# Hybrid SSD and attention block: operand of the SSD half of the output projection made during the last input unit, results of the last four column blocks in tiles of the weight pool

## The chip, the cores and the metric

One core of one Trainium2 chip runs the whole program. The metric is the device time of one execution in microseconds (us); lower is better. Engines are named as in the profile: PE (matrix products), PEld (its weight loads), ACT, DVE, POOL (element-wise engines), SP (issues most DMAs).

## The reference, cut to what matters

One block of a network on 512 tokens of width 2048, all in float32. The output projection (`mixed @ w_out`) is the part that the change touches.

```python
u = rmsnorm(h, attn_norm_w)
z, xbc, dt_raw, q, kc, vc, ks, vs, kw, vw, gate_raw = split(u @ w_in)
y_ssd = ssd_mixer(z, xbc, dt_raw, ...)      # rmsnorm(y * silu(z), norm_w), width 1024
y_att = nsa_mixer(q, kc, vc, ks, vs, ...)   # three-branch attention, 16 heads of 64, width 1024
mixed = concatenate([y_ssd, y_att], -1)     # width 2048
h = h + mixed @ w_out
v = rmsnorm(h, ffn_norm_w)
h = h + (silu(v @ w_gate) * (v @ w_up)) @ w_down
return rmsnorm(h, final_norm_w)
```

## The kernel before

**Products.** Each float32 operand is split into a high part (hi) and a remainder (lo). One 128-deep slice k of a product is three matmuls of 128x128 by 128x512: hi by hi (L234), hi by lo (L235), lo by hi (L236). The moving operand stands in the tile `U`, 16 slices with a hi and a lo each (`u` in the profile's rows).

**Stages.** First come 41 input units, one for each block of 128 columns of w_in, with 16 slices each. Then come 16 output units, one for each block c of 128 columns of w_out. Output unit c covers only its first NS[c] slices (11 or 12 of 16, 8 for the last): slices 0 to 7 are the SSD half, from 8 on the attention half. The remaining slices of w_out follow as steps 0 to 15 (`run_step`; L1177 to L1179 are their matmuls), which run from another set of tiles. Gate, up and down products come last.

**Weights.** Blocks of four slices (256 KB) are loaded on SP's queue (L200) into `wraw` tiles of the pool `wp`, tag "raw", four buffers. ACT makes `whi` (L125), DVE makes `wlo` (L128). Splits run three blocks ahead of PE, loads three blocks further. The steps load their weights into `Z` (L1112 on SP), ACT and DVE split them into `R`.

**Other work.** SSD, token compression and attention are tasks in one list. PE's program runs one slice, then `sch.tick()` lets each task go on if its count of slices is over (`yield n` waits n slices). So the attention of the last group of heads runs between the slices of the first output units. PE takes its instructions in the order in which they are written; on the other engines a scheduler places them. An engine takes its queue strictly in order.

**The SSD half of the operand.** `pre_out` runs ahead of output unit 0. For each k of 0 to 7 it loads a 256 KB slice `gy_d[k]` from memory on SP's queue (L967) into a tile `gy` of the same four "raw" buffers as the weights, POOL multiplies it by a row (L134), ACT scales it by a column and makes the hi (L125, `u<-gy,colc`), DVE makes the lo (L970). `ma_in` does the like for the attention half, from `at_d` (L977).

**Results of output units.** `ev_os(c)` copies the sum from PSUM to a tile `h1` (L989, ACT), adds the residual x by an accumulating DMA on POOL's queue (L990), and four slices later writes `h1_d[c]` by another DMA on POOL's queue (L992); the profile shows `h1_d` and `h_d` both as `h_d`, `h1` as `h`. For c up to 14 the tile is `yz` in the attention pool `att`, one buffer; for c = 15, when that pool is closed, it is a piece of the tile `A` of the next pool. `pre_last`, ahead of output unit 15, closes `att` and opens the pool with `A`, `Z`, `R`, and `R` takes memory in which the `yz` buffer lay. Step c then loads `h1_d[c]` back (L1222), adds its own sum (L137) and writes `h_d` on POOL's queue (L1228).

Of the kernel before, what the change touches and what calls it, by code (L numbers as in the profile page):

```python
# [8 lines left out]
F32 = mybir.dt.float32  # L9
# [6 lines left out]
KD = D // 128  # L16
# [14 lines left out]
PACE_OUT = [1,2,1,2]  # L31
# [36 lines left out]
U_VS = [25, 29, 33, 37]  # L68
# [47 lines left out]
def body(ctx, tc, xT, w_in, w_out, w_gate, w_up, w_down, w1k, w1v, cols, rows, kst, out):  # L116
    nc = tc.nc
    act, dve, pool, pe = nc.scalar, nc.vector, nc.gpsimd, nc.tensor
    sch = Sched()

    def f(ap):
        return ap.bitcast(F32)

    def a_hi(dst, src, scale=1.0):
        act.activation(dst, src, AF.Copy, scale=scale)  # L125

    def lo(eng, dst, src, hi):
        eng.tensor_tensor(dst, src, f(hi), ALU.subtract)  # L128
# [4 lines left out]
    def mul(eng, o, a, b):  # L133
        eng.tensor_tensor(o, a, b, ALU.mult)  # L134
# [33 lines left out]
    pools = {}  # L168

    def open_pool(name, stack=None, **kw):  # L170
        es = ExitStack()
        pools[name] = (es, es.enter_context(tc.tile_pool(name=name, bufs=1, reuse_waits="tile", **kw)))
        return pools[name][1]
# [19 lines left out]
    raw, hi_t, lo_t = {}, {}, {}  # L193
# [78 lines left out]
    def col(c, n=1):  # L272
        return colc[:, c:c + n]
# [25 lines left out]
    U = up.tile([128, 2, KD, 512], F32R, name="u")  # L299
    wp = open_pool("wp", side="right")  # L300
# [282 lines left out]
    P2 = {}  # L583
# [333 lines left out]
    def win(u):  # L917
        return w_in[u]

    ev = {U_DTG: ev_dtg}  # L920
# [28 lines left out]
    order = [U_DTG]  # L949
# [3 lines left out]
    for g in range(4):  # L953
        z = {0: [], 1: [4, 5], 2: [6], 3: [7]}[g]
        order += [U_Z[t] for t in z] + [U_VS[g], U_KS[g]] + U_Q[g]
    units = [Unit(win(u), KD, u_rhs, ev[u], pre=pre_att if u == U_VS[0] else None) for u in order]


    def pre_out():
        P2["pace"] = PACE_OUT  # L960
        sch.run_until(*[("gy", t) for t in range(8)])
        P2["ms"] = [(U[:, 0, k], U[:, 1, k]) for k in range(8)]
        P2["ma"] = [(U[:, 0, 8 + k], U[:, 1, 8 + k]) for k in range(8)]
        for k in range(8):
            h_, l_ = P2["ms"][k]
            t = wp.tile([128, 512], F32, tag="raw", name="gy", bufs=4)
            nc.sync.dma_start(t, gy_d[k])  # L967
            mul(pool, t, t, P2["row2"])
            a_hi(h_, t, scale=col(C_SN + k))
            dve.scalar_tensor_tensor(l_, t, col(C_SN + k), f(h_), op0=ALU.mult, op1=ALU.subtract)  # L970
        sch.add(ma_in(P2["at"] + 1))

    def ma_in(n):

        for k in range(n):
            h_, l_ = P2["ma"][k]
            nc.sync.dma_start(f(l_), at_d[k])  # L977
            yield 1 if k < 4 else 8
            a_hi(h_, f(l_))
            lo(dve, l_, f(l_), h_)  # L980
            sch.flags.add(("ma", k))

    def ev_os(c):
        def ev(p):
            if "att" in pools:
                t = pools["att"][1].tile([128, 512], F32, tag="yz", name="h1", bufs=1)
            else:
                t = P2["TT"][:, 2 * (c % 2):2 * (c % 2) + 2].rearrange("p a t -> p (a t)")
            act.activation(t, p, AF.Copy)  # L989
            nc.gpsimd.dma_start(t, xT[c], accum_op=ALU.add)  # L990
            yield 4
            nc.gpsimd.dma_start(h1_d[c], t)  # L992
        return ev

    def os_rhs(k):
        if k >= 8:
            assert ("ma", k - 8) in sch.flags
        return (P2["ms"] + P2["ma"])[k]

    def pre_last():  # L1000
# [10 lines left out]
    for c in range(KD):  # L1011
        units.append(Unit(w_out[c][:, 0:NS[c], :], NS[c], os_rhs, ev_os(c),
                          pre={0: pre_out, KD - 1: pre_last}.get(c)))
# [752 lines left out]
    for k in range(KD):  # L1766
        if k % 4 == 0:
            issue_split(k // 4)
        t = xt[:, k, :]
# [5 lines left out]
    for k in range(KD):  # L1775
        t = xt[:, k, :]
# [125 lines left out]
```

## Time and profile before

| | |
|---|---|
| runs, us | 2260.8, 2263.28, 2266.31 |
| median, us | 2263.28 |
| profiled execution, us | 2260.72 |
| its span, us | 2259.0 |
| mean granted PE clock | 0.984 |
| last input unit, us from the span's start | about 600 to 612 |
| output units | 614 to 829 |
| steps 0 to 15 | from 836 |

All positions below are microseconds from the start of the span. The profile has one row for one or several equal instructions: start, duration, engine, line, operation, tiles, shape, and in brackets how long the engine had been idle before it and on what that idle time ended. A granted clock of 1.00 is full speed of PE, 0.50 is half.

### The profile page before, as it was taken

What the parts mean: (1) busy time and instruction counts of PE and PEld (TensorE: products, weight loads), DVE (VectorE), ACT (ScalarE), POOL (GpSimd) and SP (SyncE); (2) the same over time, 40 slices, a digit from 0 to 9 for tenths busy, and PEclk for the clock granted to TensorE, in tenths of its full rate; (3) what the DMA queues carried; (4) which work ended last, traced back from release to release, by engine and by line L of the source; (5) the groups of instructions that cost most, each with busy time, mean ns of one, the idle gap of its engine ahead of it and who ended that gap; (6) DMA issues with size and microseconds to landing.
All of it is one profiled execution on the core that took longest, in us unless ns stands there. A gap on an engine that the chain in (4) does not pass through costs nothing. (4 is left out here: it accounts for less than half of the span.)

```text
span 2259.0 us, 34978 instructions
## 1 busy us (share of the span) xinstructions
PE 2173.3 (96%) x12892; PEld 1908.9 (85%) x12892; DVE 1799.4 (80%) x2821; ACT 1196.9 (53%) x1991; POOL 435.3 (19%) x439
## 2 busy tenths in 40 slices
PE   7999999999989989999999999999999899999996
PEld 5888888888778877888888888888888889999996
DVE  7699766778786638988888888888887878888896
ACT  4564456666666636655555555555555433433453
POOL 2011224323331116100000000000000121221232
PEclk8999999999979999999999999999999999999999
DMA  5222343222234357787878888888887869696975
GB/s 177 89 71 75 121 150 101 78 81 73 86 87 116 105 149 228 216 235 220 240 217 251 230 237 234 219 243 218 250 230 228 322 217 312 179 292 170 306 185 139
DMA packets 170492, 416.66 MB, mean 184 GB/s; under 512 B 16800, under 2 KB 23984, under 8 KB 170320
## 3 DMA queue, kind: packets, MB, share of 16 engines
q1 hardware_dynamic: 98912, 246.73, 33.4%
q0 software_dynamic: 28112, 80.65, 18.5%
q10 hardware_dynamic: 43296, 87.04, 10.6%
q8 instruction: 101, 1.65, 0.3%
q14 instruction: 71, 0.58, 0.1%
HBM read 353.54 MB, written 57.15 MB: 182 GB/s over the span
## 5 line engine op out<-in xcount | busy, mean ns | idle before, releaser
L125 ACT ACTIVATE R<-Z 128x1024 fp32r<-128x1024 f32 (+4 forms) x458 | 415.9, 922 | 449.0 <-DVE Z L137 314.6
L128 DVE TENSOR_TENSOR R<-Z,R 128x1024 fp32r<-128x1024 f32 (+4 forms) x367 | 385.5, 1059 | 42.7 <-ACT R L125 35.0
L234 PE MATMUL ps_g<-u,whi 128*128 128x512 f32 x778 | 317.5, 408 | 3.9 <-ACT u L125 3.9
L235 PE MATMUL ps_g<-u,whi 128*128 128x512 f32 x778 | 308.3, 396 | 2.7 <-DVE u L970 2.6
L236 PE MATMUL ps_g<-u,wlo 128*128 128x512 f32 x778 | 308.9, 397 | 0.0
L1173 PE MATMUL ps_s<-u,R 128*128 128x512 f32 (+1 forms) x1160 | 253.1, 348 | 9.2 <-ACT A L1383 9.0
L128 DVE TENSOR_TENSOR wlo<-wraw,whi 128x512 fp32r<-128x512 f32 x211 | 158.4, 752 | 81.5 <-ACT whi L125 79.5
L1173 PEld LDWEIGHTS ps_s<-u,R 128*128 128x128 f32 x1160 | 187.6, 188 | 41.5 <-ACT A L1383 15.1
L125 ACT ACTIVATE whi<-wraw 128x512 fp32r<-128x512 f32 x211 | 132.0, 625 | 145.5 <-PE ps_g L235 97.2
L236 PEld LDWEIGHTS ps_g<-u,wlo 128*128 128x128 f32 x778 | 147.2, 189 | 30.4
L234 PEld LDWEIGHTS ps_g<-u,whi 128*128 128x128 f32 x778 | 147.8, 190 | 29.2 <-ACT u L125 4.4
L235 PEld LDWEIGHTS ps_g<-u,whi 128*128 128x128 f32 x778 | 147.6, 190 | 29.4 <-DVE u L970 5.7
L1173 PE MATMUL ps_t<-u,R 128*128 128x512 f32 (+1 forms) x600 | 131.4, 347 | 0.0
L1173 PE MATMUL ps_g<-u,R 128*128 128x512 f32 x584 | 131.3, 349 | 0.0
L1173 PE MATMUL ps_s<-T,R 128*128 128x512 f32 (+1 forms) x560 | 125.7, 349 | 1.6 <-DVE R L128 1.6
L1173 PE MATMUL ps_g<-T,R 128*128 128x512 f32 (+1 forms) x584 | 125.7, 346 | 0.0
L1173 PE MATMUL ps_s<-V,R 128*128 128x512 f32 (+1 forms) x568 | 123.6, 347 | 1.4 <-ACT V L125 1.1
L125 ACT ACTIVATE R<-A 128x1024 fp32r<-128x1024 f32 (+3 forms) x76 | 71.0, 934 | 86.6 <-DVE A L137 61.5
L128 DVE TENSOR_TENSOR E<-Z,R 128x1024 fp32r<-128x1024 f32 (+1 forms) x91 | 111.5, 1225 | 1.4 <-ACT R L125 1.0
L137 DVE TENSOR_TENSOR A<-ps_g,A 128x512 f32<-128x512 f32 (+1 forms) x110 | 71.1, 653 | 50.8 <-PE ps_g L1173 39.1
L1173 PEld LDWEIGHTS ps_t<-u,R 128*128 128x128 f32 x600 | 98.0, 188 | 14.1
L137 DVE TENSOR_TENSOR Z<-Z 128x1024 f32<-128x1024 f32 (+5 forms) x96 | 104.2, 1085 | 6.9 <-POOL E L137 3.9
(490 smaller groups left out, 5622.9 us busy)
## 6 DMA issues: line engine op xcount, KB each, us to landing
Z<-in_w_up SPq DMA_DIRECT2D x94, 512.0 KB, 5.3
Z<-in_w_gate SPq DMA_DIRECT2D x94, 512.0 KB, 6.5
wraw<-in_w_in SPq DMA_DIRECT2D x164, 256.0 KB, 2.6
g_d<-A ACTq DMA_DIRECT2D x22, 1792.0 KB, 15.1
Z<-in_w_up POOLq DMA_DIRECT2D x37, 512.0 KB, 8.5
Z<-in_w_gate POOLq DMA_DIRECT2D x37, 512.0 KB, 7.5
Z<-in_w_down SPq DMA_DIRECT2D x59, 320.0 KB, 5.5
Z<-in_w_down SPq DMA_DIRECT2D x41, 384.0 KB, 4.1
```

The source lines that it names most:

```text
L125: act.activation(dst, src, AF.Copy, scale=scale)
L128: eng.tensor_tensor(dst, src, f(hi), ALU.subtract)
L137: eng.tensor_tensor(o, a, b, ALU.add)
L234: pe.matmul(p, hi_t[i][:, j, :], ah, start=(k == 0), stop=False)
L235: pe.matmul(p, hi_t[i][:, j, :], al, start=False, stop=False)
L236: pe.matmul(p, lo_t[i][:, j, :], ah, start=False, stop=(k == u.nk - 1))
L1173: pe.matmul(o, w, x, start=start, stop=(k == n - 1 and o is q), skip_group_check=not fresh[0])
```

## The change

The eight SSD slices are no longer made in `pre_out`. When the last input unit starts, a task `ms_in` is added, which makes slice k two ticks after slice k-1. `os_rhs` now asserts that slice k has been made when PE's program asks for it. `ev_os` puts the results of c = 12 to 15 into a "raw" buffer of `wp`; those up to 11 stay in `yz`. Lines from 957 on move by up to 8: L967 becomes L969, L970 L972, L977 L985, L989 L997, L990 L998, L992 L1000; lines of the steps move by 7 (L1112 to L1119, L1177 to L1184, L1222 to L1229, L1228 to L1235).

```diff
-    units = [Unit(win(u), KD, u_rhs, ev[u], pre=pre_att if u == U_VS[0] else None) for u in order]
-    def pre_out():
-        P2["pace"] = PACE_OUT
-        sch.run_until(*[("gy", t) for t in range(8)])
+    units = [Unit(win(u), KD, u_rhs, ev[u], pre=pre_att if u == U_VS[0] else (lambda: pre_ms()) if u == order[-1] else None) for u in order]
+    def pre_ms():
         P2["ms"] = [(U[:, 0, k], U[:, 1, k]) for k in range(8)]
-        P2["ma"] = [(U[:, 0, 8 + k], U[:, 1, 8 + k]) for k in range(8)]
+        sch.add(ms_in())
+
+    def ms_in():
+        assert "r2" in sch.flags
         for k in range(8):
+            yield 2
             h_, l_ = P2["ms"][k]
             t = wp.tile([128, 512], F32, tag="raw", name="gy", bufs=4)
             nc.sync.dma_start(t, gy_d[k])
             mul(pool, t, t, P2["row2"])
             a_hi(h_, t, scale=col(C_SN + k))
             dve.scalar_tensor_tensor(l_, t, col(C_SN + k), f(h_), op0=ALU.mult, op1=ALU.subtract)
+            sch.flags.add(("ms", k))
+
+    def pre_out():
+        P2["pace"] = PACE_OUT
+        sch.run_until(*[("gy", t) for t in range(8)])
+        P2["ma"] = [(U[:, 0, 8 + k], U[:, 1, 8 + k]) for k in range(8)]
         sch.add(ma_in(P2["at"] + 1))
...
-            if "att" in pools:
+            if c >= 12:
+                t = wp.tile([128, 512], F32, tag="raw", name="h1", bufs=4)
+            else:
                 t = pools["att"][1].tile([128, 512], F32, tag="yz", name="h1", bufs=1)
-            else:
-                t = P2["TT"][:, 2 * (c % 2):2 * (c % 2) + 2].rearrange("p a t -> p (a t)")
             act.activation(t, p, AF.Copy)
...
-        if k >= 8:
-            assert ("ma", k - 8) in sch.flags
+        assert (("ma", k - 8) if k >= 8 else ("ms", k)) in sch.flags
```

The order of instructions moves in two places. The first is the border between the last input unit and output unit 0. On POOL, before (`uq`, `ro` and `sw` are attention's query work, `at` an attention result):

```order
L128 TENSOR_TENSOR uq<-qt,uq 64x512 x2
L134 TENSOR_TENSOR gy<-gy,row_5629 128x512
L715 DMA sw_3156<-qt 8x512
L716 DMA sw_3156<-qt 8x512
L715 DMA sw_3156<-qt 8x512
L716 DMA sw_3156<-qt 8x512
L134 TENSOR_TENSOR gy<-gy,row_5629 128x512
L896 DMA at_d<-at 128x512
L134 TENSOR_TENSOR ro_6328<-sw_3158,kc 128x512
L134 TENSOR_TENSOR gy<-gy,row_5629 128x512
L128 TENSOR_TENSOR uq<-qt,uq 64x512
```

and after:

```order
L128 TENSOR_TENSOR uq<-qt,uq 64x512 x2
L134 TENSOR_TENSOR gy<-gy,row_5629 128x512 x4
L715 DMA sw_3156<-qt 8x512
L716 DMA sw_3156<-qt 8x512
L715 DMA sw_3156<-qt 8x512
L716 DMA sw_3156<-qt 8x512
L134 TENSOR_TENSOR gy<-gy,row_5629 128x512 x2
L896 DMA at_d<-at 128x512
L134 TENSOR_TENSOR ro_6333<-sw_3158,kc 128x512
L128 TENSOR_TENSOR uq<-qt,uq 64x512
```

Four of the eight multiplications now stand ahead of the four `sw` DMAs (one before), six ahead of the next `uq` (three before), and the last two a few rows behind it.

On SP the loads of the slices move up between the loads of weights (`wraw`) and of attention results (`u<-at_d`); `-` rows stand before only, `+` rows after only:

```order
 L200 DMA wraw<-in_w_out 128x384
-L200 DMA wraw<-in_w_out 128x512 x2
-L977 DMA u<-at_d 128x512 x2
+L969 DMA gy<-gy_d 128x512 x2
+L985 DMA u<-at_d 128x512 x2
+L200 DMA wraw<-in_w_out 128x512
+L985 DMA u<-at_d 128x512
+L969 DMA gy<-gy_d 128x512 x2
+L200 DMA wraw<-in_w_out 128x512
+L969 DMA gy<-gy_d 128x512 x2
 L200 DMA wraw<-in_w_out 128x384
```

Two blocks of weights of output unit 1 that were loaded ahead of all the slices are now loaded behind some, the first behind slices 0 and 1, the second behind slices 0 to 3; all go through the same four buffers.

On PE the first slices of output unit 0 move up into the attention work of the last input unit (`ps_s` are its scores, `ps_v` its products with the values):

```order
 L236 MATMUL ps_g<-u,wlo 128x512
+L234 MATMUL ps_g<-u,whi 128x512
+L235 MATMUL ps_g<-u,whi 128x512
+L236 MATMUL ps_g<-u,wlo 128x512
+L234 MATMUL ps_g<-u,whi 128x512
 L834 MATMUL ps_s<-kh,rq 128x384
 L835 MATMUL ps_s<-kl,rq 128x384
 L879 MATMUL ps_v<-pth,v 128x512
+L235 MATMUL ps_g<-u,whi 128x512
+L236 MATMUL ps_g<-u,wlo 128x512
 L879 MATMUL ps_v<-ptl,v 128x512
```

Slice 0 and slice 1 are now written ahead of this head's scores and products; from slice 2 on, PE's order is the same in both programs: slice 2 stands behind a set of 16 small matmuls of the query work, which needs the `uq` that POOL makes.

The second place is the passage from output unit 15 to step 0. On ACT, before (`h1_8458` is the result of c = 13, `h1_8507` of 14, `A_8516` here takes that of 15):

```order
L989 ACTIVATE h1_8458<-ps_g_8378 128x512
L125 ACTIVATE whi_8479<-wraw_8415 128x512
L989 ACTIVATE h1_8507<-ps_g_8461 128x512
L1222 DMA A_8516<-h1_d_66 128x512 x3
L125 ACTIVATE R_8518<-Z_8517 128x640
L989 ACTIVATE A_8516<-ps_g_8537 128x512
L125 ACTIVATE R_8518<-Z_8517 128x640
```

and after:

```order
L997 ACTIVATE h1_8458<-ps_g_8378 128x512
L1229 DMA A_8516<-h1_d_66 128x512 x3
L125 ACTIVATE whi_8479<-wraw_8415 128x512
L125 ACTIVATE R_8518<-Z_8517 128x640 x2
L125 ACTIVATE R_8518<-Z_8517 128x512 x2
L997 ACTIVATE h1_8507<-ps_g_8461 128x512
L125 ACTIVATE E_8523<-Z_8517 128x512
L997 ACTIVATE h1_8566<-ps_g_8537 128x512
```

Before, the first `R<-Z` waits for the write of c = 14 (`yz` lay where `R` lies), and the copy of c = 14 waits for the write of c = 13 (one buffer). After, the first `R<-Z` waits for the write of c = 11, four of them stand ahead of the copy of c = 14, and that copy waits for no write. POOL's queue now has the two accumulating DMAs of c = 14 and 15, then their two writes, then the first write of `h_d` (L1235).

## The prediction, made before the changed kernel had run

> **What bounds the kernel now.** I read the page's first section, then its slices, then a table of windows around the two places that the change touches, then the timeline of each engine there.
>
> ```profile
> span 2259.0 us, 34978 instructions
> PE 2173.3 (96%) x12892; PEld 1908.9 (85%) x12892; DVE 1799.4 (80%) x2821; ACT 1196.9 (53%) x1991; POOL 435.3 (19%) x439
> ...
> PE   7999999999989989999999999999999899999996
> ...
> PEclk8999999999979999999999999999999999999999
> ```
>
> PE is busy 96% of the span, so a time can only fall where PE idles or runs at a lower clock. A slice is 56.5 us. Two of the few slices in which PE is below 9 are the twelfth (621 to 678, where the clock is also 0.7) and the fifteenth (791 to 847). These hold the start of output unit 0 and the passage to the steps. The windows (PE, PEld, DVE, ACT, POOL busy, granted clock, DMA share, GB/s):
>
> ```profile
> 590.00:612.00 22.00, 22.00 (x117) 18.72 (x115) 16.57 (x46) 17.12 (x40) 8.15 (x8) 1.00 0.33 104
> 612.00:652.00 40.00, 31.97 (x110) 24.63 (x110) 35.65 (x67) 19.84 (x46) 23.45 (x19) 0.62 0.31 87
> ...
> 829.00:842.00 13.00, 5.90 (x16) 4.25 (x15) 2.73 (x4) 3.53 (x7) 1.43 (x2) 0.61 0.73 206
> ```
>
> The last input unit (590 to 612) has PE full at full clock, with DVE idle 5.4 us and POOL 13.9. Then PE runs 110 matmuls in 40 us at a clock of 0.62, against 117 in 22 us before that: at the rate of the first window (0.19 us a matmul) that is about 21 us of work, so some 19 us are lost. In this window DVE is 89% busy and POOL more than half. The passage at 829 to 842 has 5.9 us of PE in 13.
>
> **Part 1: the SSD slices earlier.** The rows of these slices, from one answer on the tile `gy`, and where PE stood:
>
> ```profile
> L134 POOL TENSOR_TENSOR gy<-gy,row x8: 1270/1364/1752, 612.1 to 641.7; 128x512 f32<-128x512 f32 x8
> L125 ACT ACTIVATE u<-gy,colc x8: 705/710/722, 613.4 to 644.2; 128x512 fp32r<-128x512 f32 x8
> L970 DVE SCALAR_TENSOR_TENSOR u<-gy,colc,u x8: 650/744/1560, 615.4 to 645.2; 128x512 fp32r<-128x512 f32 x8
> ...
>   POOL gy L134: 10.7, 4
> ...
> DMA to landing us min/median/max: 2.7/2.7/2.8
> ```
>
> ```profile
> 614.16 0.50 PE L234 MATMUL ps_g<-u,whi 128*128 128x512 f32 x1 [1.54 <-ACT u L125]
> ...
> 629.29 0.34 PE L776 MATMUL ps_m<-kch,uq 128*128 128x32 f32 x1
> ...
> 632.46 0.37 PE L777 MATMUL ps_m<-kcl,uq 128*128 128x32 f32 x1
> ...
> 640.78 0.79 PE L234 MATMUL ps_g<-u,whi 128*128 128x512 f32 x1 [2.35 <-ACT u L125]
> ...
> 644.48 0.80 PE L235 MATMUL ps_g<-u,whi 128*128 128x512 f32 x1 [0.78 <-DVE u L970]
> ...
> 651.74 0.40 PE L236 MATMUL ps_g<-u,wlo 128*128 128x512 f32 x1
> ```
>
> Today the eight slices are made between 612.1 and 645.9, each by 2.7 us of load, 1.27 to 1.75 on POOL, 0.71 on ACT, 0.74 on DVE; POOL waits 10.7 us for loads. PE waits for them at 614, 640 and 644, and unit 0 ends at 652.1.
>
> After, four POOL multiplications stand ahead of the four `sw` DMAs, which ran at 614.33 below. They move into the last input unit, 4 x 1.27 = 5.1 us in POOL's 13.9 idle, with 4 x 0.71 on ACT (4.9 idle) and 4 x 0.74 = 3.0 on DVE (5.4 idle): cost nothing, covered by a full PE whose operands are split three blocks ahead. If that cover fails, each microsecond that DVE lacks is one of PE. The eight loads pass two weight blocks on SP; those are wanted by unit 1, after 640, some 20 us after they land: nothing.
>
> The next bound is `uq`, which releases the 16 small matmuls at 629 to 632:
>
> ```profile
> 614.33 0.53 POOL L715 DMA_DIRECT2D sw<-qt  x1 [0.98 <-DVE qt L134]
> ...
> 624.21 1.62 POOL L128 TENSOR_TENSOR uq<-qt,uq 64x512 fp32r<-64x512 f32 x1 [2.41 <-ACT uq L125]
> ...
> 627.32 1.61 POOL L128 TENSOR_TENSOR uq<-qt,uq 64x512 fp32r<-64x512 f32 x1
> ```
>
> The `uq` at 624.21 waits for ACT, and that for attention work on DVE, which loses one 0.74 us operation ahead of it; the multiplications do not hold it. I let the pair move up by 1 us, so `uq` is there at 627.9 instead of 628.9 and the small matmuls end at 631.8 instead of 632.8. From slice 2 on PE's order is as before; slices 2 to 10 are 27 matmuls, 0.23 us apart at full clock (828.65 and 828.88 below), 6.2 us, with 1.7 for the scores and transposes between them, and 1 us because the clock is still low at the start: 640.7. That is 11.4 earlier than 652.1. DVE's attention work is then the next thing late: the last two slices' lo and the attention's own operations still share it, and two lo operations (2 x 0.7 = 1.4) come off the gain. **Term: 10 us.** From below: only three of the eight lo operations leave the stretch in which DVE is full, 3 x 0.74, about 2 us; nothing excludes that. From above: the 19 us of the window. A loss is possible only as rival E. I take the value that follows from the chain of rows, between the two.
>
> **Part 2: results of c = 12 to 15 in the weight pool.** Copies and DMAs are the same in number; only what they wait for changes, so their own cost is nothing. The chain at the passage:
>
> ```profile
> 828.65 0.39 PE L235 MATMUL ps_g<-u,whi 128*128 128x512 f32 x1
> 828.88 0.39 PE L236 MATMUL ps_g<-u,wlo 128*128 128x512 f32 x1
> 836.37 0.80 PE L1177 MATMUL ps_g<-u,R 128*128 128x512 f32 x1 [7.10 <-ACT R L125]
> ...
> 841.66 0.43 PE L1177 MATMUL ps_g<-u,R 128*128 128x512 f32 x1
> ```
>
> ```profile
> 818.25 0.63 ACT L125 ACTIVATE whi<-wraw 128x512 fp32r<-128x512 f32 x1 [1.60 <-issue]
> 825.58 0.60 ACT L989 ACTIVATE h<-ps_g 128x512 f32<-128x512 f32 x1 [6.69 <-DMA h_d<-h]
> 825.60 1.30 ACTq L1222 DMA_DIRECT2D A<-h_d  x3
> 835.58 0.74 ACT L125 ACTIVATE R<-Z 128x640 fp32r<-128x640 f32 x1 [9.40 <-DMA h_d<-h]
> ```
>
> ```profile
> 814.25 1.75 SPq L1112 DMA_DIRECT2D Z<-in_w_out  x4
> ...
> 826.47 0.87 POOL L990 DMA_DIRECT2D h<-in_xT  x1 [3.07 <-ACT h L989]
> 832.39 0.56 POOL L992 DMA_DIRECT2D h_d<-h  x1 [5.05 <-DMA h<-in_xT]
> 837.10 0.87 POOL L990 DMA_DIRECT2D A<-in_xT  x1 [4.15 <-ACT A L989]
> 842.39 0.56 POOL L992 DMA_DIRECT2D h_d<-A  x1 [4.42 <-DMA A<-in_xT]
> 843.58 0.54 POOL L1228 DMA_DIRECT2D h_d<-A  x1 [0.62 <-DVE A L137]
> ```
>
> ACT waits 6.69 us for the write of c = 13 into the one buffer, copies c = 14, and waits 9.40 us for its write before it may fill `R`; PE idles 7.10 us. The Z loads were issued at 814.25 to 816.0, and such loads land about 4 us later, so the data are there at 820. After, the first `R` waits only for the write of c = 11, long past, and stands behind the `whi` of 818.25 (0.63 us): four `R` and their lo parts are made by about 823, six ahead of PE's need at 829.3. The idle 7.10 goes. With it goes the slow clock: the 12 matmuls from 836.37 take 5.29 us, against 12 x 0.23 = 2.8, so 2.5 more. Together 9.6, the upper bound.
>
> The Trainium skill ("TensorE: Matmul & The Clock Gate", What's actually happening) says that after an idle window of about 3.4 us the array is at half rate until some 3.4 us of sustained work have passed. By that the half-rate stretch would cost an estimated 1.7 us instead of 2.5; the trace's 5.29 us stretch is longer, and the sum does not use the page.
>
> What is late next is POOL's queue: the copy of c = 15 comes at about 829.9, its accumulating DMA takes 0.87 to issue, and the write waits some 5 us for it (832.39 and 842.39: 5.05 and 4.42 idle), so it is issued at 836 and the first `h_d` write behind it at 836.4 instead of 843.58: 7.2 earlier, not 9.6. That write's loss of 2.4 counts only if somebody waits for it soon; POOL's sums for the steps stand behind it. **Term: 8 us**, between 7.2 and 9.6 and nearer the POOL row. If another wait takes the place of R, it is about 1.
>
> **Sum.** 10 + 8 = 18 us off the profiled execution, 2260.72 to 2242.7. The profiled execution is 2.56 below the median of 2263.28, so I predict the median at 2245.3. Some 0.2% (4.5 us) is what a measurement here can tell from no change.
>
> **The rivals.** *A, as above*: 2239 to 2251 (part 1 between 5 and 15, part 2 between 7.2 and 9.6).
>
> *B, the start of unit 0 stays with DVE and POOL.* PE at 618 to 640 waits for attention's softmax on DVE as much as for slices, and DVE is slowed while POOL multiplies:
>
> ```profile
> 618.19 3.84 DVE L849 TENSOR_SCALAR e<-e,em,gat 128x256 f32<-128x256 f32 x2
> ...
> 657.12 0.41 DVE L849 TENSOR_SCALAR e<-e,em,gat 128x256 f32<-128x256 f32 x1
> ```
>
> Two such operations took 3.84 us beside POOL's multiplications, and one takes 0.41 where POOL is quiet. Moved ahead, the multiplications would do the same to DVE in the last input unit, and unit 0 would gain only 2: 2263.3 - 2 - 8 = 2253. Against it: POOL has one multiplication fewer at 620. The Trainium skill ("GPSIMD Engine Reference", Specifications) has GpSimd and VectorE share their SBUF interfaces, which speaks against the change; the 3.84 against 0.41 agrees.
>
> *C, the whole stall goes*: if PE never loses its clock at 612 to 652, 19 + 9.6 or about 29: 2234. For it: PE is at 1.00 up to 612. Against: DVE's 89%.
>
> *D, the passage keeps a wait* (the `Z` loads or POOL's writes): 10 + 1, 2252. Against: PE's wait names R alone, and R's data were 15 us old.
>
> *E, slower: the weights starve.* Slices and results take turns in four buffers with the weights, so a weight load may wait for a slice's lo. A block that comes too late costs a load, a `whi` and a `wlo`:
>
> ```profile
> L128 DVE TENSOR_TENSOR wlo<-wraw,whi 128x512 fp32r<-128x512 f32 x211 | 158.4, 752 | 81.5 <-ACT whi L125 79.5
> L125 ACT ACTIVATE whi<-wraw 128x512 fp32r<-128x512 f32 x211 | 132.0, 625 | 145.5 <-PE ps_g L235 97.2
> ...
> wraw<-in_w_in SPq DMA_DIRECT2D x164, 256.0 KB, 2.6
> ```
>
> That is 2.6 + 0.63 + 0.75 = 4.0 us a block. Eight slices and four results could hold back up to twelve blocks; from five on (20 us) the gain of 18 is gone, and at seven it is slower: 2263.3 - 18 + 28 = 2273. Against it: blocks are loaded six ahead of their use, some 16 us at 12 matmuls of 0.23 each.
>
> **Chances.** A 0.62, B 0.16, C 0.06, D 0.06, E 0.05, and 0.05 for both parts worth nothing (2263, a wait in another place). The time is A's. The range for 8 in 10 reaches to B and D with their own uncertainty of the runs, and cuts C, E and no change: 2236 to 2257. Faster by over 0.2% is A, B, C and D, 0.90; the same 0.05; slower 0.05.
>
> **What would show it.** Right: the first slices' L134 on POOL before 612; the last matmul of unit 0 near 641 and a granted clock near 0.8 between 612 and 641; no wait of PE for `u L972`; at the passage, no idle of PE above 1 us, `R<-Z` on ACT near 819 and the clock at 1.00. Wrong: a wait of PE for `whi` or `wlo` (E), an unchanged end of unit 0 with DVE full (B), a wait of ACT or PE for a DMA at the first step (D).

## The result, and the profile after

The changed kernel took 2243.43 us (median of 4 runs, 2242.34 to 2245.78) against 2262.04 before (4 runs): a ratio of 0.992 with a 95% interval of 0.9897 to 0.9942. Two more comparisons on other chips gave 0.9949 (0.9932 to 0.9966) and 0.993 (0.9909 to 0.9951). The mean of the three is 0.9933, or 15 us. The forecast was 18 us, a median of 2245.3 and a range of 2236 to 2257.

The page's head, busy times and slices of the changed kernel:

```profile
span 2241.8 us, 34995 instructions
PE 2167.7 (97%) x12892; PEld 1908.6 (85%) x12892; DVE 1794.5 (80%) x2821; ACT 1196.4 (53%) x1991; POOL 432.3 (19%) x439
...
PE   7999999999999999999999999999999899999996
...
PEclk9999999999979999999999999999999999999998
```

PE's two slices below 9 around the change are gone (the twelfth and the fifteenth), but the clock of the twelfth is still 0.7. The windows of the same places:

```profile
590.00:612.00 22.00, 22.00 (x116) 18.87 (x115) 19.05 (x47) 17.67 (x41) 11.57 (x12) 1.00 0.38 120
612.00:652.00 40.00, 31.75 (x136) 26.32 (x135) 37.40 (x85) 25.49 (x59) 19.85 (x18) 0.70 0.30 86
...
829.00:842.00 13.00, 13.00 (x58) 10.43 (x57) 10.36 (x16) 8.71 (x16) 10.23 (x15) 1.00 0.77 252
```

The last input unit takes up the moved work (DVE 19.05 of 22 instead of 16.57) and PE stays full. In 612 to 652 PE runs 136 matmuls instead of 110, but DVE is now busy 37.4 of 40. The passage, which before idled here, is full.

To see where the time went, count PE's 12892 matmuls in order of their starts and take the time between the same two of them in each profile. Five stretches follow one another: matmul 3000 (in the last input unit) to 3300 (early in output unit 3), on to 4027 (six matmuls before the end of unit 15), on to 4048 (in step 0), on to 4500 (past the steps), and on to the last, in us. Unit 0 ends with matmul 3127, unit 1 with 3213 and unit 2 with 3276; the texts on record below that call matmul 3300 the end of unit 1 mean this stretch.

| profile | 3000 to 3300 | to 4027 | to 4048 | to 4500 | to the last |
|---|---|---|---|---|---|
| before | 77.2 | 142.6 | 14.6 | 97.7 | 1308.5 |
| changed | 72.2 | 142.6 | 4.9 | 96.6 | 1308.2 |
| changed, second and third | 72.0, 70.2 | 142.6 | 4.9 | 97.5, 98.0 | 1311.8, 1309.4 |

So part 1 is worth 5.0 to 7.0 us in the first of them and part 2 9.8 at the passage. Nothing moves between them. The last column, in which the kernels do not differ, varies by 3.6 us from profile to profile of the same kernel.

**The start of unit 0.** From the tile `gy`, and from PE's timeline:

```profile
L134 POOL TENSOR_TENSOR gy<-gy,row x8: 1275/1302/1754, 602.7 to 631.6; 128x512 f32<-128x512 f32 x8
L972 DVE SCALAR_TENSOR_TENSOR u<-gy,colc,u x8: 730/746/1395, 606.8 to 636.4; 128x512 fp32r<-128x512 f32 x8
```

```profile
616.16 0.50 PE L834 MATMUL ps_s<-kh,rq 128*128 128x512 f32 x1 [3.20 <-DVE em L838]
...
628.75 0.39 PE L776 MATMUL ps_m<-kch,uq 128*128 128x32 f32 x1 [1.23 <-POOL uq L128]
...
641.46 0.40 PE L236 MATMUL ps_g<-u,wlo 128*128 128x512 f32 x1
643.21 0.49 PE L879 MATMUL ps_v<-pth,v 128*128 128x512 f32 x1 [1.36 <-ACT pth L125]
...
648.83 1.09 PE L863 MATMUL ps_t<-ident,e 128*128 128x128 f32 x4 [1.09 <-DVE em L847]
```

PE no longer waits for a slice. Unit 0 ends at 641.9, against 652.1 (this profile was already 0.8 us ahead in the last input unit). Its waits are now attention's: 3.20 us for a score on DVE, 1.23 for `uq`, and 1.36 and 1.09 right behind unit 0. What DVE did ahead of the first:

```profile
612.42 1.76 DVE L128 TENSOR_TENSOR wlo<-wraw,whi 128x512 fp32r<-128x512 f32 x1
...
614.36 1.40 DVE L972 SCALAR_TENSOR_TENSOR u<-gy,colc,u 128x512 fp32r<-128x512 f32 x2
615.68 0.41 DVE L838 CUSTOM_DVE_ANT_0 e<-ps_s,kc 128x256 f32<-128x256 f32 x1
```

Two lo operations of the moved slices (1.40 together) stand ahead of the score for which PE waits.

Where the gain lies can be read from the whole stretch from matmul 3000 to 3300, before, in the first and in the third profile of the changed kernel:

```profile
607.71:684.90 77.19, 67.82 (x303) 54.83 (x301) 64.94 (x157) 48.36 (x116) 27.28 (x24) 0.80 0.33 91
606.87:679.04 72.17, 63.92 (x302) 53.52 (x301) 62.45 (x157) 48.27 (x116) 23.58 (x22) 0.83 0.34 100
609.65:679.87 70.22, 62.37 (x302) 52.19 (x301) 62.41 (x157) 47.94 (x116) 23.18 (x22) 0.85 0.35 103
```

The matmuls are the same. PE's idle time falls from 9.4 us to 8.3 and 7.9 only; the rest of the 5.0 and 7.0 us is busy time, which falls because the clock is higher: it is at half for 30.7 us before, 23.9 in the first profile and 20.5 in the third. (With part 2 alone, a kernel that is as before in this stretch, PE idles 10.3 and 11.2 us and the clock is at half for 27.3.) So part 1 gains by idle time and by the clock, in shares that change from profile to profile: idle time is 1.1 to 1.5 us of it against the profile before, and 2.1 to 3.4 against the two of part 2 alone.

**The passage.** PE, ACT and POOL:

```profile
823.03 0.39 PE L236 MATMUL ps_g<-u,wlo 128*128 128x512 f32 x1
823.25 0.39 PE L1184 MATMUL ps_g<-u,R 128*128 128x512 f32 x1
```

```profile
812.93 1.88 ACT L125 ACTIVATE R<-Z 128x640 fp32r<-128x640 f32 x3
815.76 0.63 ACT L125 ACTIVATE R<-Z 128x512 fp32r<-128x512 f32 x1 [0.95 <-DMA Z<-in_w_out]
818.07 0.60 ACT L997 ACTIVATE h<-ps_g 128x512 f32<-128x512 f32 x1 [1.68 <-PE ps_g L236]
```

```profile
829.16 0.56 POOL L1000 DMA_DIRECT2D h_d<-h  x1 [1.11 <-DMA h<-in_xT]
829.71 0.54 POOL L1235 DMA_DIRECT2D h_d<-A  x1
```

The step's first matmul starts 0.22 us after the last of unit 15. The last of these four `R<-Z` ended at 816.4, some 7 us ahead of it. The first write of the steps (L1235) still stands behind the write of c = 15, 6.5 us after PE's first step, and no wait of PE over 0.5 us follows before 870.5.

### The profile page after: what moved, and what is told of

Read it like the earlier page. It is cut to its first block, busy times and chain, and to the rows that moved or that the text cites. A ratio compares the mean times of both kernels' runs of the same rounds, so it can differ in the third digit from the quotient of the medians.

```text
span 2241.8 us, 34995 instructions
## 1 busy us (share of the span) xinstructions
PE 2167.7 (97%) x12892; PEld 1908.6 (85%) x12892; DVE 1794.5 (80%) x2821; ACT 1196.4 (53%) x1991; POOL 432.3 (19%) x439
```

## The experiments

**Each part alone.** Theory: the two parts act in different places and add. Rivals stand in the texts that follow. The first program is the changed kernel with the result tiles of before, so that only the earlier slices are left of the change:

```diff
-            if c >= 12:
-                t = wp.tile([128, 512], F32, tag="raw", name="h1", bufs=4)
+            if "att" in pools:
+                t = pools["att"][1].tile([128, 512], F32, tag="yz", name="h1", bufs=1)
             else:
-                t = pools["att"][1].tile([128, 512], F32, tag="yz", name="h1", bufs=1)
+                t = P2["TT"][:, 2 * (c % 2):2 * (c % 2) + 2].rearrange("p a t -> p (a t)")
```

> The SSD slices in the last input unit as in the changed kernel, the results of the output units in the tiles of before. Theory (the two parts act in different places and add): PE is 5 us ahead of the kernel before from output unit 1 on (10 ahead at the end of unit 0, 4 to 5 given back right behind it), and the idle 7 us and the slow clock at the first step stay, about 2.5 more: the time is about 5 us below before, 2257. Rival (the parts depend on each other, because a later passage only shifts the wait): the gain is gone at the first step, 2262.

The second has the new `ev_os` in the old kernel:

```diff
-            if "att" in pools:
+            if c >= 12:
+                t = wp.tile([128, 512], F32, tag="raw", name="h1", bufs=4)
...
```

> The results of c = 12 to 15 in tiles of the weight pool, the SSD slices made as before. Theory: PE is level with before up to the end of output unit 15 and 9.8 us ahead from the first step on (7.1 of idle and 2.5 of slow clock), 2252. Rival (POOL's queue, where the write of c = 15 stands ahead of the first write of the steps, gives part of it back): 7.2, 2255.

Part 2 alone: ratio 0.9955 (0.9938 to 0.9971), some 10 us, and 0.996 (0.9947 to 0.9974) when it was repeated. Part 1 alone: 0.9998 (0.9984 to 1.0013), nothing. The repeats:

> The results of c = 12 to 15 in tiles of the weight pool alone, once more, on the chip of the run of the changed kernel. Theory: stretch to the end of unit 1 of 76 to 77 us, passage of 4.9 us, steps of 50 to 56 us, time about 10 below before. Rival: steps of 50 to 51 us again, 3 or more below those of every kernel with part 1.

> The SSD slices in the last input unit alone, once more, for a second profile. Theory (its local gain of 7 us is real, and the steps, whose order of instructions on DVE, ACT and POOL came out otherwise in this program, give it back every time): 69 to 73 us to the end of unit 1, and 102 us or more from the first step on to matmul 4500, against 96 to 98 in all the other kernels; time the same as before. Rival (that stretch was slow in one profile by chance): 96 to 99 us there, and the time is 4 us or more below before.

Part 1 alone again gave 1.0001 (0.9984 to 1.0017). The stretches:

| profile | 3000 to 3300 | to 4048, from 4027 | to 4500 |
|---|---|---|---|
| before | 77.2 | 14.6 | 97.7 |
| part 1 alone | 69.8, 70.0 | 15.3, 14.3 | 103.3, 100.7 |
| part 2 alone | 76.6, 76.8 | 4.9, 4.9 | 95.6, 96.3 |
| both (three profiles) | 70.2 to 72.2 | 4.9 | 96.6 to 98.0 |

Locally each part does what it does in the changed kernel: 7 us at the start of unit 0, 9.8 at the passage. But without part 2 the gain of part 1 shrinks in the steps, by 5.6 us and, in the repeat, 3.0 against before; the repeat, at 100.7, lies below the 102 that its text expected. At matmul 4500 the repeat and the first profile are still 4.7 and 1.8 us ahead of the one of before, so the steps account for part of the missing gain only; the rest is not found in a stage, and the times vary by more than that from run to run. At the passage of part 1 alone PE waits as before:

```profile
829.38 0.80 PE L1184 MATMUL ps_g<-u,R 128*128 128x512 f32 x1 [8.08 <-ACT R L125]
```

and in the steps it idles again, and its clock falls (windows, columns as above):

```profile
873.00:883.00 10.00, 6.10 (x25) 4.65 (x26) 5.18 (x8) 5.47 (x9) 4.72 (x7) 0.94 0.98 269
883.00:893.00 10.00, 10.00 (x36) 8.02 (x37) 8.53 (x11) 5.14 (x9) 7.37 (x10) 0.72 0.36 120
```

The largest waits there, DVE's and PE's:

```profile
882.05 0.69 DVE L137 TENSOR_TENSOR A<-ps_g,A 128x512 f32<-128x512 f32 x1 [3.57 <-DMA A<-h_d]
882.80 0.80 PE L1184 MATMUL ps_g<-u,R 128*128 128x512 f32 x1 [3.77 <-DVE A L137]
```

DVE waits 3.57 us for the load of a result (4.06 in the repeat), and PE waits 3.77 behind it (2.14). The DMA share of 0.98 and a DVE near its limit in the windows around it show a stage with little room. Such waits of DVE are not special to this program, though: the three profiles with both parts have them too, of 1.1 to 3.4 us. In this program the order of DVE's, ACT's and POOL's instructions in the steps came out otherwise (POOL has a write of `h_d` ahead of the write of c = 15), while it is the same with part 2 alone and with both. A kernel further down (c = 14 and 15 only), whose ACT and POOL orders in the steps also differ, took 99.9 us there. That the order costs the 3 to 6 us is only argued: no run changed it alone. That the parts do not add is what the times say: 0 and 10 us alone, 15 together. By the intervals I estimate some 4 us of uncertainty for this difference of 5, so it stands just clear of noise. The rival for part 2 (POOL's queue gives some back) fell: 9.8 is all of the idle time and the slow clock, and the stretch behind it, to matmul 4500, takes 95.6 and 96.3 us, not more than the 97.7 of before.

**The changed kernel again**, beside the others:

> The changed kernel once more, for a second profile and a closer time beside the kernel with only the second part. Theory (part 1 gains locally 5 to 7.5 us, which of the two is set by whether PE's clock falls to half in unit 1): the stretch from the last input unit's end to the end of unit 1 is 69.5 to 72.5 us against 77 before, the steps 0 to 15 take 50 to 56 us whatever the kernel, and the time is 5 us below that of the kernel with part 2 alone. Rival (part 1 is given back in the steps, as in the kernel with part 1 alone): the steps take 3 us or more longer than with part 2 alone, and the times differ by less than 3.

> The changed kernel a third time, on the chip of the three others. Theory: 72 us to the end of unit 1, passage 4.9, 96 to 98 from the first step on to matmul 4500; 12 to 18 us below before, and 2 to 3 above the kernel with the scaling on ACT. Rival: within 1 us of that kernel.

Ratios 0.9949 and 0.993, stretches in the tables. The rival of the first text came half: the steps took at most 2.4 us longer than with part 2 alone, in the same order, but the times on that chip differ by 1.3 us only (2248.8 and 2250.0); the last stretch, in which the kernels are the same, was 3.7 us longer in this profile. Over all comparisons the kernel with both parts is 15 us below before and the one with part 2 alone 9.6 (the mean of 10.2 and 9.0). So part 1 brings about 5 when part 2 is there, but only 1.3 where the two were timed on one chip; its size is not settled better than that. The third profile missed its text's 72 us (70.2), and its time is 0.9 us above the kernel with the scaling on ACT further down (2246.1 and 2245.2), which is that text's rival.

Up to the passage, PE, DVE, ACT, POOL and SP have the same order in the changed kernel, in part 1 alone and in the kernel with c = 14 and 15 only. Their six profiles show 72.2, 72.0, 70.2, 69.8, 70.0 and 69.8 us from matmul 3000 to 3300. The windows of the first and of the third profile, behind unit 0:

```profile
645.00:648.00 3.00, 2.74 (x14) 2.23 (x12) 2.07 (x9) 2.95 (x9) 0.94 (x1) 0.52 0.28 87
648.00:651.00 3.00, 2.17 (x8) 1.91 (x9) 2.21 (x10) 2.10 (x7) 0.19 (x1) 0.50 0.62 87
```

```profile
645.00:648.00 3.00, 1.70 (x10) 1.25 (x9) 2.53 (x8) 2.94 (x7) 0.00 (x0) 1.00 0.27 87
648.00:651.00 3.00, 1.55 (x13) 1.24 (x12) 2.76 (x12) 2.95 (x9) 0.94 (x1) 1.00 0.26 87
```

The waits are alike (1.36, 0.23 and 1.09 us; 1.08, 0.22 and 1.51), but in the first the clock halves. From matmul 3128, the first behind unit 0, to 3300 the two profiles with the low clock take 35.8 us and the four with the high one 33.7: 2.1 us hang on the clock.

**What bounds the start of unit 0.** Two kernels leave work out, to see what PE's waits there are made of. These two and the last kernel below (c = 14 and 15 only) ran once each (2242.5, 2240.7 and 2243.7 us), too few to compare times, so their stretches are read.

```diff
-            mul(pool, t, t, P2["row2"])
```

> The changed kernel without POOL's eight multiplications of the SSD slices by the row; all else stays. Theory (POOL slows DVE beside it): the DVE operations at 612 to 622 that took 1.76, 1.35 and 1.85 us fall to 0.7, 0.4 and 0.3, the row of 16 small matmuls starts 3 us earlier, PE's idle 3.2 us at the start of unit 0 shrinks below 2, and unit 1 begins 3 to 4 us earlier than in the changed kernel. Rival (DVE has too much work there, whoever stands beside it): unit 1 begins at most 1 us earlier.

```diff
-            dve.scalar_tensor_tensor(l_, t, col(C_SN + k), f(h_), op0=ALU.mult, op1=ALU.subtract)
```

> The changed kernel without DVE's eight lo operations of the SSD slices (the lo slices keep older values). Theory (DVE's own amount of work is the limit at the start of unit 0): two of them, 1.4 us, stand ahead of the score that ends PE's wait of 3.2 us, so that wait falls to about 1.8, and the whole 8 x 0.74 = 6 us come off the stretch up to unit 1, which begins 4 to 6 us earlier. Rival (contention with POOL): unit 1 begins 1 to 2 us earlier.

Without POOL's multiplications, PE and DVE:

```profile
618.55 0.50 PE L834 MATMUL ps_s<-kh,rq 128*128 128x512 f32 x1 [3.26 <-DVE em L838]
```

```profile
616.81 0.68 DVE L128 TENSOR_TENSOR wlo<-wraw,whi 128x512 fp32r<-128x512 f32 x1
```

Without DVE's lo operations:

```profile
616.77 0.50 PE L834 MATMUL ps_s<-kh,rq 128*128 128x512 f32 x1 [1.96 <-DVE em L838]
```

Without POOL's multiplications `wlo` shrinks as the theory had it (1.76 to 0.68), but the wait stays (3.26), unit 1 does not begin earlier, and the stretch is 69.7 us, against 69.8 to 70.2 for the changed program at high clock: 0.5 at most. So the rival holds. Contention is real in the single operations. What it costs the path this kernel does not show cleanly, since DVE's order came out otherwise in it: five lo operations now stand ahead of the score instead of four, which takes back most of what `wlo` saved. Without the lo operations the wait falls to 1.96 (1.8 was forecast), and the stretch to 66.7: 3.1 to 3.5 less, with 6 us taken off DVE. Unit 1 begins 1.0 to 2.7 us earlier than in the six profiles above, nearer the rival's 1 to 2 than the theory's 4 to 6. Part of this gain is again the clock, which is at half for 13.7 us of the stretch instead of 20.5. What PE waits for at the start is what DVE has to do ahead of attention's scores.

**Three ways to use that.** First, slices loaded directly:

```diff
-            nc.sync.dma_start(t, gy_d[k])
-            mul(pool, t, t, P2["row2"])
+            nc.sync.dma_start(f(l_), gy_d[k])
+            mul(pool, t, f(l_), P2["row2"])
```

(with `yield 1` for `yield 2`).

> The changed kernel, but the SSD slices are loaded into their own lo places of the operand as soon as PE has read them, one slice a tick, and only the product of POOL's multiplication takes a tile of the weight ring. All eight loads stand ahead of the second group of weight loads, and all eight multiplications ahead of the query work on POOL. Theory (the four buffers shared with the weights hold the loads back to 626 and with them the multiplications to 631): the last multiplication ends before 622 instead of 633, and the stretch to the end of unit 1 falls by 3 to 5 us against the changed kernel, to 67 to 69. Rival (DVE's amount of work is the limit, not when the slices arrive): it falls by less than 1, or rises, since eight multiplications now slow DVE in the last input unit.

```profile
616.05 4.50 POOL L134 TENSOR_TENSOR gy<-u,row 128x512 f32<-128x512 f32 x3
...
618.57 0.80 PE L834 MATMUL ps_s<-kh,rq 128*128 128x512 f32 x1 [4.44 <-DVE em L838]
```

All multiplications end at 620.6, nearly 13 us earlier, and PE's wait grows to 4.44: five lo operations stand ahead of the score instead of four, and the last of them takes 1.75 us beside POOL's multiplications. The stretch is 71.0. The rival holds. The time is 0.9932 of before (0.9914 to 0.995), not to be told from the changed kernel's 0.9949 on the same chip.

Second, attention at a slower pace through units 0 and 1:

```diff
+PACE_FROM = 2
...
+    def pre_pace():
+        P2["pace"] = PACE_OUT
...
-        P2["pace"] = PACE_OUT
...
-                          pre={0: pre_out, KD - 1: pre_last}.get(c)))
+                          pre={0: pre_out, PACE_FROM: pre_pace, KD - 1: pre_last}.get(c)))
```

> The changed kernel, but the attention work keeps the slower pace of the input units (2, 2, 2, 3 slices an item) through output units 0 and 1 and takes the faster one (1, 2, 1, 2) from unit 2 on. Theory (DVE is full at the start of unit 0 and PE waits for attention's softmax): PE has more slices to run between the items, the waits of 3.2 and 1.4 us shrink, the stretch to the end of unit 1 holds less attention work and is 3 to 6 us shorter, the later units take up the same work at full clock, and 2 to 4 us stay. Rival (what PE waits for at 613 to 632 was written ahead of unit 0 whatever the pace): nothing changes before unit 1 and the time is the same within 1 us, or the attention ends too late for the passage and it is slower by some us.

```profile
617.27 0.80 PE L835 MATMUL ps_s<-kh,rq 128*128 128x512 f32 x1 [3.39 <-DVE em L839]
```

The first wait stays and the stretch is 70.5, no less than at high clock without the edit. PE's order is another in this kernel, so the stretch does not hold quite the same matmuls; from the end of the last input unit, unit 2 ends after 62.8 us (63.1 to 63.5 at high clock without the edit) and unit 15 after 212.2 (211.3 to 211.8), so what is gained first is given back later. The time is 0.9954 (0.9937 to 0.9971): the rival again.

Third, part of DVE's work moved to ACT:

```diff
-                if br:
+                if br and "ms" not in P2:
                     dve.tensor_scalar(e[:, 0:L], ...
```

> The changed kernel, but from the last input unit on the scaling of the second branch's softmax (L849, on DVE 0.4 to 1.35 us each beside POOL) is made by ACT, as that of the first branch is, with one small product more on DVE (0.16). Theory (DVE's amount of work bounds the start of unit 0): 2 to 3 us of DVE's work go between 612 and 642, the stretch to the end of unit 1 falls from 72 to 68 to 70 us and the time by 2 to 3. Rival (ACT, on which the exponentials wait, becomes as late as DVE): the stretch stays at 72 or grows.

```profile
612.00:642.00 30.00, 24.52 (x104) 20.88 (x103) 28.34 (x58) 18.64 (x42) 18.67 (x17) 0.66 0.28 90
```

DVE is still busy 28.3 of 30 us, the stretch is 69.8, as the changed program at high clock has it, and the time 0.9928 (0.9908 to 0.9949), against 0.993 for the changed kernel beside it. It gains nothing that can be measured: the 2 to 3 us of the theory did not come. The small product that takes the place of the scaling (0.15 us at 614.5) took 1.16 and 1.78 us at 618.9 and 620.1, beside POOL, and DVE's busy time in this window is only 0.6 to 1.2 us below that of the changed program (28.9 to 29.6). None of the three beats the changed kernel by more than the noise.

**Which results matter at the passage.**

```diff
-            if c >= 12:
+            if c >= 14:
```

> The changed kernel with only the results of c = 14 and 15 in tiles of the weight pool; c = 12 and 13 stay in the one buffer. Theory (what cost the 9.8 us is the write of c = 14 that had to wait for the buffer and then held up R): R now waits for the write of c = 13, which lands some 2 us after it was issued, 3 to 4 us ahead of PE's need; the passage takes 4.9 us as with all four. Rival (the whole chain of copies, accumulations and writes is late, one result behind the other): PE idles 2 us or more at the first step and the passage takes over 7.

```profile
817.22 0.60 ACT L997 ACTIVATE h<-ps_g 128x512 f32<-128x512 f32 x1 [5.05 <-PE ps_g L236]
...
819.10 2.41 ACT L125 ACTIVATE R<-Z 128x640 fp32r<-128x640 f32 x4 [1.28 <-DMA h_d<-h]
```

The copy of c = 14 waits for PE alone. `R` waits 1.28 us for a write, that of c = 13, and is made between 819.1 and 821.5, 0.9 us ahead of PE's first step at 822.4 (3 to 4 were expected). The passage takes 4.9 us. So the theory holds: moving the results of c = 14 and 15 removes the whole cost, and by the wait of ACT before, which ended on the write of c = 14, it is c = 14 in the single buffer. c = 14 was not moved alone.

## Why the prediction was right, and where not

- **Sum.** 18 us were forecast and 18.6 measured first, but the mean of three comparisons is 15, and the local stretches give 14.8 (5.0 + 9.8) in the first profile. The time is in the range, with two terms wrong in opposite ways; that the first time came so near is luck.
- **Part 1, forecast 10, measured 5.0 (7.0 to 7.4 where the clock held).** The chain up to the end of unit 0 was right in the main: the multiplications ahead of the `sw` DMAs ran from 602.7 to 613.6, and unit 0 ended at 641.9, 9.4 us earlier net of the head start of 0.8, of the 11.4 forecast. Two sizes were off by 1.0 us each. The small matmuls behind `uq`, which was there at 628.7 (forecast 627.9), end no earlier than before net of the head start. And slices 2 to 10 took 9.9 us instead of 8.9: the clock was low until 634.9 (granted 0.71 between 612 and 641, where near 0.8 was the sign of being right). The step that failed is the allowance for DVE, two lo operations or 1.4 us. In its place PE waited for attention behind unit 0 and its clock fell, which gave back 4.4 us in unit 1 (10.3 ahead at its start, 5.9 at its end). In the four profiles without the clock's fall 0.9 to 2.0 were given back. PE, which no longer waits for the slices, only comes to its next wait sooner.
- **A wait was added that the prediction did not have:** 3.20 us at 616, of which the moved lo operations ahead of a score make 1.2 (it is 1.96 without them). Before, three waits of 1.54, 0.37 and 0.41 stood there. DVE's queue had been counted for its idle time (5.4 us) and not for its order.
- **Part 2, forecast 8, measured 9.8.** The upper bound (9.6) was right to 0.2: the idle 7.1 us and the slow clock both went. The mis-sized term is what I gave to POOL's queue, 2.4 us, of which the term kept 1.6. It cost nothing; the late write was there (6.5 us behind PE's first step), but no wait of PE over 0.5 us came in the 47 us behind that step.
- **Rivals.** B is right that the start stays with DVE, and wrong in its price: it gave unit 0 a gain of 2 us, and 9.4 came. Its reading of the profile before was also off: between 618 and 641 PE waited 3.3 us for slices and 0.7 for attention, not as much for one as for the other. What holds the start is DVE's work (3.1 to 3.5 us less without the lo operations). POOL's share in it stays open: without the multiplications the stretch gained 0.5 us at most, with DVE's order changed. The Trainium skill ("GPSIMD Engine Reference", Specifications) says that GpSimd shares SBUF interfaces with VectorE: the single operations agree (1.76 against 0.68 us). C did not come, D and E neither: between 612 and 830 PE had no wait over 0.2 us for `whi` or `wlo`.
- **Not foreseen:** that the parts depend on each other. Part 1 alone moves the time by nothing that can be measured.

## What to carry to other kernels

Before a step is moved ahead on an engine's queue, look at what stands behind it there and who waits for that, not only at the idle time of the engine: two operations of 0.7 us ahead of the wrong score cost PE 1.2 us of waiting. A result buffer that is the memory of the next stage should be given up first by the last writers; two results in another pool removed the whole 9.8 us. And a gain measured locally need not be kept in the stages behind it: time each part alone and both.

## What the runs showed of the hardware

The clock's fall is not fixed by the program. The same instructions behind unit 0 kept a clock of 1.00 in four profiles and fell to 0.50 in two, with waits of 2.8 and 2.7 us in all in the two shown above; the fall is worth 2.1 us. Within each of the 14 profiles all changes of the clock lie on one grid with a step of 3.41 us (to 0.01 us), and where this grid lies against the work differs from profile to profile. The Trainium skill ("TensorE: Matmul & The Clock Gate", What's actually happening) describes a free-running window of about 3.4 us, which agrees with that. Its default after an idle window does not fit as it stands: in the two profiles with the fall no single wait behind unit 0 was longer than 1.4 us, and PE was busy for about half of the time ahead of the fall at 645.1, whether the window is cut at 3 us or on the grid:

```profile
642.00:645.00 3.00, 1.56 (x8) 1.21 (x9) 2.53 (x8) 2.94 (x7) 0.00 (x0) 1.00 0.27 87
641.70:645.10 3.40, 1.81 (x10) 1.31 (x10) 2.93 (x10) 3.06 (x7) 0.00 (x0) 1.00 0.24 77
```

In the two profiles with the fall one window of the grid held both early waits, and PE was busy 53% and 52% of it; in the four others the waits were spread over more windows, and none was below 56%. So the place of the grid is the likely reason for the difference. No limit can be read off from it: in the other programs, at 570 to 700 us, single windows of 47 to 53% kept the clock, and three of 66 to 92% lost it.
